# Small operands of the reciprocal roots and of the rows' maxima placed in unused columns of PSUM banks

## The chip, the cores and the metric

The kernel runs on one core of a Trainium2 chip, in one launch. The metric is the device time of one execution in microseconds, here 2229.23 us as the median of three runs (2226.55 to 2230.64).

The engines by the names of the profile: PE multiplies matrices (PEld are its weight loads), DVE is VectorE, ACT is ScalarE, POOL is GpSimd, SP issues the DMAs. SBUF is the memory on the chip that all of them work in. PSUM holds eight banks of 512 f32 columns on 128 partitions, into which PE writes its products; ACT and DVE read them from there. Each engine runs its own instructions in order and waits at semaphores for those of other engines.

## The reference

Two layers of a streaming encoder work on 1152 tokens (1024 of a prompt, and 8 requests of 16 samples) of 1024 channels, in f32. Layer 0 has a sliding-window attention and a recurrent branch (RG-LRU) side by side, layer 1 a gated MLP over chunks of 128 tokens; an MLP with a squared ReLU follows each.

```python
def rms_norm(x, g):
    xf = x.astype(jnp.float32)
    y = xf * lax.rsqrt(jnp.mean(xf * xf, axis=-1, keepdims=True) + EPS)
    return (y * g.astype(jnp.float32)).astype(x.dtype)
...
def softmax_with_sink(s, sink):
    sk = sink.astype(jnp.float32)[:, :, None, None]
    m = jnp.maximum(jnp.max(s, axis=-1, keepdims=True), sk)
    e = jnp.exp(s - m)
    return e / (jnp.sum(e, axis=-1, keepdims=True) + jnp.exp(sk - m))
...
    q = rope(rms_norm(q, q_g), pos)
    k = rope(rms_norm(k, k_g), pos)
...
    xc, new_buf = causal_conv(xr, conv_buf, conv_w, conv_b)
    hs, new_h = rg_lru(xc, h0, wa, ba, wx, bx, lam)
    rec = hs * jax.nn.gelu(gr)
    out = jnp.concatenate([att, rec], axis=-1) @ w_out
```

The reciprocal roots of the change are those of `rms_norm`: over the 1024 channels of a token ahead of each layer and each MLP, and over the 64 channels of each head of q and k. The rows' maxima are `jnp.max(s)` of the softmax.

## The kernel before

Every f32 product is made of three in a narrower format: weights and activations are split into a high part, rounded, and a low part, the rest (`three`, L526 to L528: high by high, low by high, high by low). The high part of a weight is a copy by ACT (`w<-raw`, L200), the low one a subtraction by DVE (L201); activations are split in `norm_split` (ACT L522, DVE L523). Weights come from HBM by DMA into `raw` in the order in which they are used.

The channels are laid on the partitions, and the tokens along the columns in three blocks of 384 (`nb`). These stages follow each other, with the times of the profile:

- **The start (0 to about 165 us).** The list `START` names the first steps: `n` splits a piece of x, `s` squares it and adds it to the sum over the channels, `w` splits a weight, `m` a projection, `f` is `stat_tokens`, `F` is `spread_stat`, `e` moves a projection out of PSUM. `stat_tokens` (L479) sums the squares over the partitions by three matmuls with one column each, into columns 0 to 2 of a bank of the kind `ax`, computes 1/1024 of that plus epsilon into the buffer `small`, and calls `rsqrt` (L446), which leaves the root of three times 128 tokens in `rT`. `spread_stat` (L495) turns it by PE into rows, and DVE copies them into `rstd`. Then the recurrent branch runs over four blocks of 128 channels (order in `LRU_ORDER`): projections, a causal convolution over 1176 columns (`add_conv`, L573), gate matmuls into `ax` banks (L526, `ax<-xch,w`), sigmoids and exponentials by ACT, a scan along the time by DVE (L644), and the product with a gelu. `prepare_lru` (L546) makes the constants `spc` of the decay out of 25 small instructions, also in `small`.
- **The attention (165 to 345 us).** Nine tiles of 128 tokens. `tile_steps` (L801) handles one of them: ACT copies q (eight heads of 64) and k and v out of two banks of the kind `mm` into `raw`, scaled; POOL squares q and k (ten heads); DVE sums each head (`tensor_reduce`), then takes ten roots per token by shift, subtraction from a constant, and three steps of Newton; POOL works meanwhile on the rotary embedding; DVE scales, and the result is split, transposed by PE and used for the scores. `prompt_steps` (L937) handles two heads of a tile: scores into a bank of the kind `qk`, DVE takes the maxima `mx` and from them the negative bound `nm`, ACT the exponentials with their sums, DVE the reciprocal, POOL the product, PE transposes, ACT and DVE split (`pT`), PE multiplies by v (`pv`), ACT and DVE split the result (`xn0h`, `xn0l`).
- **The out-projection** with the residual (to about 428 us), the statistics of the sum, and the **MLP**, whose products (L1293) take two thirds of the time. Then **layer 1**, from 1120 us on: gated MLP, out-projection, MLP. Their roots come from `stat_tokens` (L1152, L1184) and, for the layer norm of the gated MLP, from `rsqrt` with operands in SBUF.

What sets the order: a scheduler places the instructions of the start, the out-projections and the MLPs on each engine by its own estimate of when their inputs are ready, so that a changed dependence reorders others. In the attention the calls go through `InOrder`, which keeps the order in which the program makes them on each engine (all such instructions carry the line L257). That order is given by hand: `TILE_AT`, `REC_AT` and `PAIR_AT` list the due time of each step of a tile, of the recurrent rest and of a pair of heads; a step ends at each `yield`, and the steps of all of them are sorted by due time. A buffer can be written anew when its last reader has finished; so can a bank. Three `mm` banks serve q, and k and v, in turn.

The small operands of the root of a tile are ten columns each in one SBUF tile `st8`:

```python
        ss, v, y, w = (st8[:, 10 * i:10 * i + 10] for i in range(4))
```

(in the profile `st`), and those of the softmax are pairs of columns in `m`. The bank of k and v is filled in its first 256 columns of 512 (`kv_mm`); in a bank of scores columns 192 to 255 stay unused, since a chunk's scores take 192 (`pwide`).

Of the kernel before, what the change touches and what calls it, by code (L numbers as in the profile page):

```python
# [12 lines left out]
I32 = mybir.dt.int32  # L13
AF = mybir.ActivationFunctionType
OP = mybir.AluOpType
# [4 lines left out]
P = 128  # L20
# [261 lines left out]
def body(ctx, tc, io):  # L282
    nc = tc.nc
# [96 lines left out]
    q, kv = io["wq"], io["wkv"]  # L380
# [62 lines left out]
    rT = cp.tile([P, TT], F32, name="rT")  # L443
    small = cp.tile([P, 3, 16], F32, name="small")

    def rsqrt(y, v, t):  # L446

        yi, vi = y.bitcast(I32), v.bitcast(I32)
        nc.vector.tensor_scalar(yi, vi, 1, None, OP.logical_shift_right)
        nc.vector.tensor_scalar(yi, yi, -1, 0x5F3759DF, OP.mult, OP.add)  # L450
        for _ in range(3):
            nc.vector.scalar_tensor_tensor(t, y, -0.5, y, OP.mult, OP.mult)
            nc.vector.tensor_mul(t, t, v)
            nc.vector.scalar_tensor_tensor(y, t, 1.5, y, OP.add, OP.mult)


    ssum = {}
# [21 lines left out]
    def stat_tokens(nb, tag="ax"):  # L479

        s = ssum.pop(nb)
        ps = bank(tag)
        n = NBW // P
        for t in range(n):
            nc.tensor.matmul(ps[:, t:t + 1], s[:, t * P:t * P + P], ones, start=True, stop=True)
        v, w, r = small[:, 0, 0:n], small[:, 1, 0:n], rT[:, nb * n:nb * n + n]
        nc.vector.tensor_scalar(v, ps[:, 0:n], 1.0 / D, EPS, OP.mult, OP.add)
        rsqrt(r, v, w)

# [218 lines left out]
    for step in START.split():  # L708
# [11 lines left out]
        elif kind == "m":  # L720
            c, nb = n
# [6 lines left out]
    for kind, c in LRU_ORDER:  # L728
        if kind == "G":
            gates(c)  # L730
        else:
            nb = seen[kind, c] = seen.get((kind, c), -1) + 1
# [9 lines left out]
    PEo, ACTo, DVEo, POOLo = (InOrder(tc, e) for e in (nc.tensor, nc.scalar, nc.vector, nc.gpsimd))  # L742

    def at(name, shape, dt=F32, tag=None, bufs=1):
        return ap_.tile(shape, dt, tag=tag or name, bufs=bufs, name=name)
# [13 lines left out]
    raw = at("raw", [P, 12, 64])  # L759
# [6 lines left out]
    zero = pb[0][:, 0:NVV * 128].rearrange("p (n j x) -> p n j x", n=NVV, j=2)  # L766
    for a in (64, 128):
        nc.vector.tensor_copy(vv[:, :, :, a:a + 64], zero)
    st8 = at("st8", [P, 40])

    qkv = {}

# [28 lines left out]
    def tile_steps(s):  # L801
# [5 lines left out]
        r = rT[:, s:s + 1]  # L807
        ACTo.activation(raw[:, 0:8, :], qkv.pop(("q", s)).rearrange("p (h x) -> p h x", x=64), AF.Copy, scale=r)
        yield
        ACTo.activation(raw[:, 8:12, :], qkv.pop(("kv", s))[:, :256].rearrange("p (h x) -> p h x", x=64), AF.Copy, scale=r)  # L810
        yield
        qk = raw[:, 0:10, :]
        POOLo.tensor_mul(t1, qk, qk)
        yield
        ss, v, y, w = (st8[:, 10 * i:10 * i + 10] for i in range(4))
        DVEo.tensor_reduce(ss, t1, AX.X, OP.add)
        DVEo.tensor_scalar(v, ss, 1.0 / 64, EPS, OP.mult, OP.add)
        yield
# [4 lines left out]
                f = slice(32 - 32 * half, 64 - 32 * half)  # L823
                POOLo.tensor_mul(t2[:, a:b, o], qk[:, a:b, f], tab[:, i, 1:2, o].to_broadcast([P, n, 32]))
        yield
        yi, vi = y.bitcast(I32), v.bitcast(I32)
        DVEo.tensor_scalar(yi, vi, 1, None, OP.logical_shift_right)
        DVEo.tensor_scalar(yi, yi, -1, 0x5F3759DF, OP.mult, OP.add)
        for n in range(3):
            DVEo.scalar_tensor_tensor(w, y, -0.5, y, OP.mult, OP.mult)  # L830
            DVEo.tensor_mul(w, w, v)
            DVEo.scalar_tensor_tensor(y, w, 1.5, y, OP.add, OP.mult)
            if n == 1:
                yield
        yield
        for i, (a, b) in enumerate(((0, 8), (8, 10))):
            POOLo.tensor_mul(t1[:, a:b], qk[:, a:b], tab[:, i, 0:1, :].to_broadcast([P, b - a, 64]))
        yield
# [98 lines left out]
    def prompt_steps(t, i):  # L937

        kvh, pair = i % 2, i // 2
        h0 = kvh * 4 + pair * 2  # L940
        ps = bank("qk")
        p = pb[(4 * t + i) % NPB]
        qT = qTs[t % 2]
        for c in range(2):
            for a, n, pos in cells(t, c):
                o = ps[:, c * 256 + a:c * 256 + a + n]
                lhs = qT[:, c * 512 + h0 * 64:c * 512 + h0 * 64 + P]
                PEo.matmul(o, lhs, kT[:, kvh, 0, pos:pos + n], start=True, stop=False)
                PEo.matmul(o, lhs, kT[:, kvh, 1, pos:pos + n], start=False, stop=True)
        yield  # L950
        m = at(f"m{t}_{i}", [P, 8], tag="m", bufs=4)
        mx, nm, den, es = (m[:, 2 * k:2 * k + 2] for k in range(4))
        first = cells(t, 0)[0][0]
        spans = [(first, 192), (256 + max(first, 64), 512)]
        if t:
            DVEo.tensor_reduce(mx, pwide(ps), AX.X, OP.max)
        else:
            for c in range(2):
                DVEo.tensor_reduce(mx[:, c:c + 1], ps[:, spans[c][0]:spans[c][1]], AX.X, OP.max)
        DVEo.tensor_scalar(nm, mx, -0.125, nsink[:, h0 // 2:h0 // 2 + 1], OP.mult, OP.min)  # L960
        yield
        for c in range(2):
            a, b = spans[c]
            ACTo.activation(p[:, a:b], ps[:, a:b], AF.Exp, bias=nm[:, c:c + 1], scale=0.125,
                            accum_out=den[:, c:c + 1])
        ACTo.activation(es, nm, AF.Exp, bias=sink[:, h0 // 2:h0 // 2 + 1])
        yield
        DVEo.tensor_add(den, den, es)
        DVEo.reciprocal(den, den)
        yield  # L970
        if t:
            w = pwide(p)
            POOLo.tensor_mul(w, w, den.rearrange("p (c x) -> p c x", x=1).to_broadcast([P, 2, 192]))
        else:
            for c in range(2):
                a, b = spans[c]
                POOLo.tensor_scalar_mul(p[:, a:b], p[:, a:b], den[:, c:c + 1])
        yield
        pT = pTs[i % 2]
        ps = bank("tp")  # L980
        kts = (0, 1) if t else (1,)
        for kt in kts:
            for c in range(2):
                PEo.transpose(ps[:, (kt * 2 + c) * P:(kt * 2 + c + 1) * P],
                              p[:, c * 256 + kt * P:c * 256 + kt * P + P], ident)
        yield
        a = 256 * kts[0]
        ACTo.copy(pT[:, 0, a:], ps[:, a:])
        yield
        DVEo.tensor_sub(pT[:, 1, a:], ps[:, a:], pT[:, 0, a:].bitcast(F32))  # L990
        yield
        if kvh == 0:
            pv[0] = bank("pv")
        ps = pv[0]
        for kt in kts:
            vh, vl = (vv[:, (t - 1 + kt) % NVV, j, kvh * 128:kvh * 128 + 128] for j in range(2))
            ph, pl = (pT[:, j, kt * 256:kt * 256 + 256] for j in range(2))
            PEo.matmul(ps[:, :256], vh, ph, start=kvh == 0 and kt == kts[0], stop=False)
            PEo.matmul(ps[:, :256], vl, ph, start=False, stop=False)
            PEo.matmul(ps[:, :256], vh, pl, start=False, stop=kvh == 1 and kt == 1)  # L1000
        yield
        if kvh:
            src = ps[:, :256].rearrange("p (c j x) -> p j c x", c=2, j=2)
            cols = slice(t * P, t * P + P)
            o = [x[:, pair * 2:pair * 2 + 2, cols].rearrange("p j (c x) -> p j c x", c=2) for x in (xh, xl)]
            ACTo.copy(o[0], src)
        yield
        if kvh:
            DVEo.tensor_sub(o[1], src, o[0].bitcast(F32))
        yield  # L1010
# [95 lines left out]
    x = {}  # L1106
# [699 lines left out]
```

## Time and profile before

| what | us |
|---|---|
| median of three runs | 2229.23 |
| the profiled execution | 2230.83 |
| its span, first to last instruction | 2229.1 |
| PE busy in the span | 2167.5 |
| DVE busy | 1633.8 |
| ACT busy | 961.2 |
| POOL busy | 275.8 |

The span cut into 40 equal slices of some 56 us, the busy tenths of each engine in each:

```profile
PE   7988989899999999999999999989999999999999
DVE  7878984698777778777784644269877777877776
ACT  4665553367666642111152113226766665221211
POOL 4156641100000000000040333110000000000000
```

The first three slices are the start, the next three and a bit the attention and what follows it; POOL is busy there, and once more in the middle of layer 1 (slices 21 to 27). In between lie the MLPs, where PE is at nine tenths or more. How rows are read: start or count, busy time, engine, line, operation, output<-inputs, partitions x elements; a bracket gives the idle time of the engine ahead of the instruction and what ended it.

### The profile page before, as it was taken

How to read it: one execution, taken by the hardware profiler on the slowest of the kernel's cores; microseconds unless marked ns; L12 is line 12 of the kernel's file. 1: busy time of each engine (PE TensorE's matmuls, PEld its weight loads, DVE VectorE, ACT ScalarE, POOL GpSimd, SP SyncE). 2: the span in 40 equal slices, each digit the busy share in tenths (PEclk: the TensorE clock that was granted, in tenths of full speed). 3: DMA queues.
4: the chain of work that ended last, by engine and by line, in shares of the span. 5: the costliest groups of instructions: out<-in, count | busy, mean ns of one | idle time of the engine just before them, and what ended most of it. 6: DMA issues, size and time to landing. Idle time of an engine off the chain costs nothing.

```text
span 2229.1 us, 37892 instructions
## 1 busy us (share of the span) xinstructions
PE 2167.5 (97%) x14980; PEld 2120.6 (95%) x14980; DVE 1633.8 (73%) x2810; ACT 961.2 (43%) x1694; POOL 275.8 (12%) x332
## 2 busy tenths in 40 slices
PE   7988989899999999999999999989999999999999
PEld 7987889899999999999997899989999999999999
DVE  7878984698777778777784644269877777877776
ACT  4665553367666642111152113226766665221211
POOL 4156641100000000000040333110000000000000
PEclk9999999999999999999999999999999999999999
DMA  4120042227666677356652022422856667735573
GB/s 155 53 63 6 6 135 95 77 77 306 226 241 225 253 300 288 132 200 217 252 178 64 18 67 85 133 73 73 309 218 241 222 255 305 282 133 214 201 255 147
DMA packets 108002, 377.91 MB, mean 170 GB/s; under 512 B 13472, under 2 KB 24736, under 8 KB 107808
## 3 DMA queue, kind: packets, MB, share of 16 engines
q1 hardware_dynamic: 107680, 375.47, 46.9%
q8 instruction: 118, 1.93, 0.4%
q14 instruction: 60, 0.49, 0.1%
q10 hardware_dynamic: 144, 0.02, 0.0%
HBM read 240.09 MB, written 136.26 MB: 169 GB/s over the span
## 4 chain that ended last, share of the span: by engine, by line
PE 85%; DVE 9%; ACT 3%; issue 1%; DMA 1%; POOL 0%; SPq 0%; DVEq 0%; ACTq 0%; POOLq 0%
PE two L1293 64%; PE mm L527 4%; PE mm L526 4%; PE mm L528 4%; DVE st L257 2%; PE mm L1610 1%; PE mm L1612 1%; PE mm L1611 1%; PE mm L257 1%; DVE w L201 1%; DVE m L257 1%; PE pv L257 1%; PE ax L1639 1%; DVE y L573 1%; PE tp L257 1%
## 5 line engine op out<-in xcount | busy, mean ns | idle before, releaser
L1293 PE MATMUL two<-b,w 128*128 128x288 f32 x5424 | 727.8, 296 | 11.2 <-DVE x L1137 11.2
L1293 PEld LDWEIGHTS two<-b,w 128*128 128x128 f32 x5424 | 726.6, 189 | 11.7 <-issue 11.7
L1293 PE MATMUL two<-h,w 128*128 128x288 f32 x4704 | 630.6, 295 | 2.7 <-DVE x L1492 1.6
L1293 PEld LDWEIGHTS two<-h,w 128*128 128x128 f32 x4704 | 627.5, 188 | 4.5 <-issue 2.3
L200 ACT CAST w<-raw 128x512 fp32r<-128x512 f32 x542 | 331.7, 621 | 645.3 <-PE two L1293 435.8
L201 DVE TENSOR_TENSOR w<-raw,w 128x512 fp32r<-128x512 f32 x542 | 377.4, 701 | 107.7 <-ACT w L200 105.8
L1492 DVE TENSOR_TENSOR x<-two,x 128x576 f32<-128x576 f32 x448 | 336.1, 754 | 130.4 <-PE two L1293 129.1
L526 PE MATMUL mm<-xn0h,w 128*128 128x384 f32 x372 | 127.9, 344 | 7.0 <-ACT xn0h L522 6.5
L527 PE MATMUL mm<-xn1l,w 128*128 128x384 f32 x372 | 125.8, 338 | 1.7 <-DVE xn1l L523 1.7
L526 PE MATMUL mm<-xn1h,w 128*128 128x384 f32 x372 | 126.0, 339 | 0.0
L528 PE MATMUL mm<-xn0h,w 128*128 128x384 f32 x372 | 126.0, 339 | 0.0
L527 PE MATMUL mm<-xn0l,w 128*128 128x384 f32 x372 | 125.9, 339 | 0.0
L528 PE MATMUL mm<-xn1h,w 128*128 128x384 f32 x372 | 125.9, 338 | 0.0
L1542 POOL TENSOR_TENSOR s<-s,tmp 128x384 f32<-128x384 f32 (+1 forms) x28 | 29.1, 1064 | 729.1 <-ACT tmp L1541 728.8
L1293 PE MATMUL two<-hk,w 128*128 128x288 f32 x672 | 91.2, 295 | 0.0
L407 DVE TENSOR_TENSOR ho<-c_a,ho 128x576 fp32r<-128x576 f32 x78 | 57.2, 753 | 46.1 <-ACT ho L406 46.1
L1293 PEld LDWEIGHTS two<-hk,w 128*128 128x128 f32 x672 | 90.1, 188 | 0.0
L526 PEld LDWEIGHTS mm<-xn0h,w 128*128 128x128 f32 x372 | 71.0, 191 | 8.6 <-ACT xn0h L522 7.4
L1322 ACT ACTIVATE c_a<-c_a 128x1152 f32<-128x1152 f32 x60 | 70.1, 1168 | 14.8 <-DVE c_a L1404 13.8
L407 DVE TENSOR_TENSOR ho<-c_b,ho 128x576 fp32r<-128x576 f32 x96 | 72.3, 753 | 3.6 <-ACT ho L406 3.6
L1137 DVE TENSOR_TENSOR x<-mm,x 128x384 f32<-128x384 f32 x48 | 26.6, 554 | 64.6 <-PE mm L528 64.5
L527 PEld LDWEIGHTS mm<-xn1l,w 128*128 128x128 f32 x372 | 70.7, 190 | 2.1 <-DVE xn1l L523 2.0
(280 smaller groups left out, 2837.2 us busy)
## 6 DMA issues: line engine op xcount, KB each, us to landing
hidden<-ho SPq DMA_DIRECT2D x196, 576.0 KB, 4.0
h<-hidden SPq DMA_DIRECT2D x196, 576.0 KB, 6.3
raw<-in_w SPq DMA_DIRECT2D x136, 512.0 KB, 4.4
x<-scratch SPq DMA_DIRECT2D x24, 576.0 KB, 7.7
scratch<-x SPq DMA_DIRECT2D x48, 192.0 KB, 1.8
raw<-in_wo SPq DMA_DIRECT2D x16, 512.0 KB, 3.7
xin<-in_xT SPq DMA_DIRECT2D x24, 192.0 KB, 4.1
x<-in_xT SPq DMA_DIRECT2D x8, 576.0 KB, 3.8
```

Source lines behind the costliest of these rows:

```text
L200: nc.scalar.copy(t[:, 0], src)
L201: nc.vector.tensor_sub(t[:, 1], src, t[:, 0].bitcast(F32))
L257: return lambda *a, **k: self.tc.keep_in_program_order(op(*a, **k))
L407: nc.vector.tensor_sub(lo, src, hi.bitcast(F32))
L526: nc.tensor.matmul(ps, wh, ah, start=start, stop=False)
L527: nc.tensor.matmul(ps, wh, al, start=False, stop=False)
L528: nc.tensor.matmul(ps, wl, ah, start=False, stop=stop)
L1137: nc.vector.tensor_add(o, ps[:, :NBW], o)
L1293: nc.tensor.matmul(o, w, a[:, c], start=first and k == 0 and i == 0, stop=k == len(pairs) - 1 and i == 2, skip_group_check=True)
L1322: nc.scalar.activation(o, o, AF.Relu) if fn == "relu" else nc.scalar.square(o, o)
L1492: nc.vector.tensor_add(o, both(ps), o)
L1542: nc.gpsimd.tensor_add(o, o, sq)
```

## The change

`rsqrt` becomes a generator, `rsqrt_steps`, that takes the engine and yields behind the second and third step of Newton, as the hand-written copy of it in `tile_steps` did. The number of instructions is the same: a shift, a multiply-and-add, and three times three. What is new is which operands they have. Before, the step was t = −y/2 · y, t = t · v, y = (t + 1.5) · y; now it is t = −y/2 · v, t = t · y, y = (t + 1.5) · y, so that each instruction has `y` and just one of `v` and `t`. And `v` and `t` move to PSUM: in `stat_tokens` to columns 8 to 10 and 16 to 18 of the bank that holds the sums (before: `small`), in `tile_steps` with the sum of squares to columns 256, 272 and 288 of the bank of k and v (before: `st8`), while `y` is an SBUF tile of its own. The maxima `mx` move to columns 192 and 193 of the bank of scores. The layer norm's call of `rsqrt` keeps its operands in SBUF.

A bank is thereby held longer: that of k and v until the root ends, that of the sums too. `small` is left to `prepare_lru` and the scans.

```diff
     def rsqrt(y, v, t):
-        yi, vi = y.bitcast(I32), v.bitcast(I32)
-        nc.vector.tensor_scalar(yi, vi, 1, None, OP.logical_shift_right)
-        nc.vector.tensor_scalar(yi, yi, -1, 0x5F3759DF, OP.mult, OP.add)
-        for _ in range(3):
-            nc.vector.scalar_tensor_tensor(t, y, -0.5, y, OP.mult, OP.mult)
-            nc.vector.tensor_mul(t, t, v)
-            nc.vector.scalar_tensor_tensor(y, t, 1.5, y, OP.add, OP.mult)
+        for _ in rsqrt_steps(y, v, t, nc.vector):
+            pass
+
+    def rsqrt_steps(y, v, t, dve):
+        dve.tensor_scalar(t.bitcast(I32), v.bitcast(I32), 1, None, OP.logical_shift_right)
+        dve.tensor_scalar(y.bitcast(I32), t.bitcast(I32), -1, 0x5F3759DF, OP.mult, OP.add)
+        for n in range(3):
+            dve.scalar_tensor_tensor(t, y, -0.5, v, OP.mult, OP.mult)
+            dve.tensor_mul(t, t, y)
+            dve.scalar_tensor_tensor(y, t, 1.5, y, OP.add, OP.mult)
+            if n:
+                yield
...
-        v, w, r = small[:, 0, 0:n], small[:, 1, 0:n], rT[:, nb * n:nb * n + n]
+        v, w, r = ps[:, 8:8 + n], ps[:, 16:16 + n], rT[:, nb * n:nb * n + n]
...
-    st8 = at("st8", [P, 40])
+    y = at("y", [P, 10])
...
-        ACTo.activation(raw[:, 8:12, :], qkv.pop(("kv", s))[:, :256].rearrange("p (h x) -> p h x", x=64), AF.Copy, scale=r)
+        kvb = qkv.pop(("kv", s))
+        ACTo.activation(raw[:, 8:12, :], kvb[:, :256].rearrange("p (h x) -> p h x", x=64), AF.Copy, scale=r)
...
-        ss, v, y, w = (st8[:, 10 * i:10 * i + 10] for i in range(4))
+
+        ss, v, w = (kvb[:, 256 + 16 * i:266 + 16 * i] for i in range(3))
...
-        yi, vi = y.bitcast(I32), v.bitcast(I32)
...
-        yield
+        for _ in rsqrt_steps(y, v, w, DVEo):
+            yield
...
-        m = at(f"m{t}_{i}", [P, 8], tag="m", bufs=4)
-        mx, nm, den, es = (m[:, 2 * k:2 * k + 2] for k in range(4))
+        m = at(f"m{t}_{i}", [P, 6], tag="m", bufs=4)
+        nm, den, es = (m[:, 2 * k:2 * k + 2] for k in range(3))
+        mx = ps[:, 192:194]
```

The lines behind the diff's first part stand five further down in the changed kernel (L523 is L528 there, L644 is L649). In the attention the order of the instructions on each engine stays. At the start the scheduler reorders. First DVE at the end of the root of the first block (`small` and `rT` are the root's operands before, `ax_301` and `rT` now; L523 splits pieces of x, L496 copies the spread root). Before:

```order
L453 TENSOR_TENSOR small<-small 128x3
L454 SCALAR_TENSOR_TENSOR rT<-small,rT 128x3
L523 SCALAR_TENSOR_TENSOR xn1l_84<-xin_101,gt,xn1h_83 128x384
L523 SCALAR_TENSOR_TENSOR xn0l_79<-xin_97,gt,xn0h_78 128x384
L496 COPY rstd_88<-ax_376 128x384
```

Now:

```order
L528 SCALAR_TENSOR_TENSOR xn1l_84<-xin_101,gt,xn1h_83 128x384
L455 SCALAR_TENSOR_TENSOR ax_301<-rT,ax_301 128x3
L528 SCALAR_TENSOR_TENSOR xn0l_79<-xin_97,gt,xn0h_78 128x384
L456 TENSOR_TENSOR ax_301<-ax_301,rT 128x3
L528 SCALAR_TENSOR_TENSOR xn1l_84<-xin_99,gt,xn1h_83 128x384
L457 SCALAR_TENSOR_TENSOR rT<-ax_301,rT 128x3
L201 TENSOR_TENSOR w_415<-raw_163,w_415 128x512
L201 TENSOR_TENSOR w_418<-raw_163,w_418 128x512
L501 COPY rstd_88<-ax_376 128x384
```

Three splits of x stand between the last instructions of the root, and two splits of a weight behind it, ahead of the copy. `prepare_lru`, which also writes `small`, stood behind the root of block 1 (from row 81 of DVE's on) and now stands ahead of it (rows 56 to 80). Next, DVE around the first scan (`h_754<-rg_722,rg_738`; `u_784` is a projection for the gelu, `pad_718` the next block's convolution input). Before:

```order
L631 SCALAR_TENSOR_TENSOR h_754<-rg_722,h_754 128x1176
L634 TENSOR_TENSOR rg_738<-rg_738,h_754 128x1176
L641 MEMSET rg_722 128x8
L640 TENSOR_TENSOR rg_738<-rg_738,small 128x8
L644 SCALAR_TENSOR_TENSOR h_754<-rg_722,rg_738 128x1176
L691 TENSOR_TENSOR u_784<-mm_864,rstd_88 128x384
L201 TENSOR_TENSOR w_517<-raw_506,w_517 128x512
L674 TENSOR_TENSOR pad_718<-mm_897,rstd_88 128x256
```

Now:

```order
L636 SCALAR_TENSOR_TENSOR h_754<-rg_722,h_754 128x1176
L696 TENSOR_TENSOR u_784<-mm_864,rstd_88 128x384
L201 TENSOR_TENSOR w_517<-raw_506,w_517 128x512
L639 TENSOR_TENSOR rg_738<-rg_738,h_754 128x1176
L201 TENSOR_TENSOR w_545<-raw_515,w_545 128x512
L201 TENSOR_TENSOR w_548<-raw_515,w_548 128x512
L645 TENSOR_TENSOR rg_738<-rg_738,small 128x8
L646 MEMSET rg_722 128x8
L679 TENSOR_TENSOR pad_718<-mm_897,rstd_88 128x256
L649 SCALAR_TENSOR_TENSOR h_754<-rg_722,rg_738 128x1176
```

The projection, three splits of weights and the padding, behind the scan before, stand ahead of it. Last, PE at the gate matmuls of the sixth bank (`ax_858`). Before:

```order
L526 MATMUL mm_897<-xn1h_83,w_464 128x384
L527 MATMUL mm_897<-xn1l_84,w_464 128x384
L526 MATMUL ax_858<-xch_814,w_503 128x392
L527 MATMUL ax_858<-xcl_816,w_503 128x392
L528 MATMUL ax_858<-xch_814,w_503 128x392
L528 MATMUL mm_897<-xn1h_83,w_464 128x384
```

Now:

```order
L531 MATMUL mm_984<-xn1h_83,w_512 128x384
L532 MATMUL mm_984<-xn1l_84,w_512 128x384
L533 MATMUL mm_984<-xn1h_83,w_512 128x384
L531 MATMUL ax_858<-xch_814,w_503 128x392
L532 MATMUL ax_858<-xcl_816,w_503 128x392
L533 MATMUL ax_858<-xch_814,w_503 128x392
L531 MATMUL mm_1017<-xn0h_78,w_545 128x384
```

They stood in the middle of the projection `mm_897`, at row 372 of PE's; they now stand at row 400, behind a whole further projection, `mm_984`. On SP the order of the DMAs is the same but for a few outputs of the cache.

More of the change, by code (lines that the diff above doesn't have):

```diff
@@ L825, in tile_steps @@
         yield
-        yi, vi = y.bitcast(I32), v.bitcast(I32)
[L827 to L833, printed above, removed]
-                yield
-        yield
+        for _ in rsqrt_steps(y, v, w, DVEo):
+            yield
         for i, (a, b) in enumerate(((0, 8), (8, 10))):
```

## The prediction

> **What bounds the kernel now.** I read the page first: the share of each engine, then the chain of work that ended last.
>
> ```profile
> span 2229.1 us, 37892 instructions
> PE 85%; DVE 9%; ACT 3%; issue 1%; DMA 1%; POOL 0%; SPq 0%; DVEq 0%; ACTq 0%; POOLq 0%
> PE two L1293 64%; PE mm L527 4%; PE mm L526 4%; PE mm L528 4%; DVE st L257 2%; PE mm L1610 1%; PE mm L1612 1%; PE mm L1611 1%; PE mm L257 1%; DVE w L201 1%; DVE m L257 1%; PE pv L257 1%; PE ax L1639 1%; DVE y L573 1%; PE tp L257 1%
> ```
>
> TensorE ends 85% of the chain, and the products of the MLPs (L1293) alone 64%; the change touches none of those. But VectorE's small instructions on `st` and `m` (L257), which it does touch, hold 3% of the chain, some 65 us. So I read next how busy the engines are in each stage. The columns are the stretch, its length, then busy time and count of PE, weight loads, DVE, ACT and POOL, then the granted clock, the DMA share and GB/s.
>
> ```profile
> 60.00:165.00 105.00, 94.27 (x510) 90.74 (x509) 81.50 (x101) 70.75 (x86) 35.76 (x30) 0.95 0.21 61
> 165.00:285.00 120.00, 109.75 (x754) 97.40 (x753) 108.39 (x276) 66.89 (x219) 75.11 (x95) 0.99 0.03 8
> 285.00:345.00 60.00, 53.87 (x341) 50.78 (x341) 51.28 (x131) 34.84 (x109) 21.23 (x25) 0.91 0.42 133
> 450.00:1120.00 670.00, 669.40 (x5019) 668.69 (x5018) 529.19 (x790) 302.36 (x467) 0.00 (x0) 1.00 0.62 229
> ```
>
> From 450 to 1120 us PE has no gap: nothing is to be won or lost there. From 165 to 285 us, in the attention, PE is idle for 120 − 109.75 = 10.25 us while VectorE is 108.4 of 120 us busy. What PE waits for there, in the waits of PE (total, times, longest):
>
> ```profile
> PE pv L257 <- DVE xn0l L257: 6.2, 5, 1.7
> PE tp L257 <- DVE xa L257: 3.5, 3, 2.1
> ```
>
> 9.7 of the 10.25 us are waits for VectorE. So in this stage VectorE sets the end, with PE close behind it. That caps the gain: however much VectorE is relieved, PE's own 109.75 us remain.
>
> **What the change does to VectorE.** The timeline of one tile's root (start, length, engine):
>
> ```profile
> 228.94 1.71 POOL L257 TENSOR_TENSOR rstd<-raw,tab 128x512 f32<-128x512 f32 x2
> 228.99 1.70 DVE L257 TENSOR_SCALAR st<-st 128x10 int32<-128x10 int32 x2
> 230.73 1.58 POOL L257 TENSOR_TENSOR rstd<-rstd,rope_b 128x640 f32<-128x640 f32 x1
> 230.92 1.42 DVE L257 TENSOR_TENSOR st<-st 128x10 f32<-128x10 f32 x1
> 232.38 0.38 DVE L257 SCALAR_TENSOR_TENSOR st<-st 128x10 f32<-128x10 f32 x2
> ```
>
> Ten elements per partition take 1.4 us as long as a POOL instruction runs: the one that starts at 230.92 ends at 232.34, just behind the POOL instruction's end at 232.31; with POOL done, two take 0.38. I look for which instructions this happens to, in the groups (count, busy us, mean ns) and in the summaries of three buffers (shortest, median and longest ns):
>
> ```profile
> L257 DVE SCALAR_TENSOR_TENSOR st<-st 128x10 f32<-128x10 f32 x54 | 21.2, 392 | 1.5
> L257 DVE TENSOR_TENSOR st<-st 128x10 f32<-128x10 f32 x27 | 11.4, 423 | 0.9
> L257 DVE TENSOR_SCALAR st<-st 128x10 int32<-128x10 int32 x18 | 9.9, 548 | 0.3
> L257 DVE TENSOR_SCALAR m<-m,nsink 128x2 f32<-128x2 f32 x32 | 14.3, 448 | 1.0
> L257 DVE TENSOR_SCALAR m<-m,nsink x32: 216/478/1000, 179.8 to 326.4; 128x2 f32<-128x2 f32 x32
> L257 DVE SCALAR_TENSOR_TENSOR st<-st x54: 148/170/1425, 166.6 to 316.9; 128x10 f32<-128x10 f32 x54
> L257 DVE TENSOR_TENSOR pT<-tp,pT x16: 410/681/693, 191.9 to 339.0; 128x512 fp32r<-128x512 f32 x14, 128x256 fp32r<-128x256 f32 x2
> ```
>
> The undisturbed price is about 168 ns (the median of the first kind is 170). Instructions with both operands in SBUF are stretched to 1425; the subtraction `pT<-tp,pT`, which has one operand in PSUM and is fifty times larger, never goes above 693 among the same POOL work. So I take it that an instruction with one operand in PSUM goes free of POOL. The change gives every instruction of the tile's root such an operand, and the maxima's `nm` too. What goes: 54 × (392 − 168) = 12.1, 27 × (423 − 168) = 6.9, 18 × (548 − 168) = 6.8, 32 × (448 − 220) = 7.3 us (220 being an undisturbed `nm`, whose shortest is 216): **33 us of VectorE's time**, 3.7 us in each of nine tiles. That is more than the waits it can end.
>
> What of it shortens the span: the 9.7 us of waits, plus slowed work just behind them:
>
> ```profile
> 206.44 0.83 PE L257 MATMUL pv<-xa,vv 128*128 128x256 f32 x5
> 252.14 1.25 PE L257 MATMUL pv<-xa,vv 128*128 128x256 f32 x6 [1.19 <-DVE xn0l L257]
> 168.30 1.58 POOL L257 TENSOR_TENSOR rstd<-rstd,rope_b 128x640 f32<-128x640 f32 x1
> 171.25 0.17 DVE L257 SCALAR_TENSOR_TENSOR st<-st 128x10 f32<-128x10 f32 x1
> ```
>
> Six of these after a stall take 1.25 us; five without one 0.83, so six would take 1.0: 0.25 us for each of the five stalls, 1.3 together. Sum 11.0. I take off 1.5. In the first tile, whose stall is the 2.1, POOL's own sum is late next: it ends at 169.88, 1.5 us before the root, so 0.6 stays. The other 0.9 is an allowance for waits behind which ACT stands. **Attention: −9.5 us**, bounds −6 (half the waits find another engine) and −14 (some of the 6.1 us that PE idles from 285 to 345 too, though those mostly wait for ACT and weights).
>
> What holds longer: the root's operands lie in the bank of k and v, which now comes free at the end of the root, not after ACT's copy. The next user of such a bank is a projection two tiles later:
>
> ```profile
> 170.80 0.63 PE L257 MATMUL mm<-w,xn0h 128*128 128x512 f32 x2
> 234.66 0.72 DVE L257 SCALAR_TENSOR_TENSOR st<-st 128x10 f32<-128x10 f32 x1
> 239.65 0.63 PE L257 MATMUL mm<-w,xn0h 128*128 128x512 f32 x2
> ```
>
> In a middle tile the root ends at 235.4, the matmuls start at 239.65: 4 us to spare. In the first tile the root ends at 171.42 (its last row is above), the matmuls start at 170.80; there they would wait 0.6 us, but about 3.5 us of stretching go before that point. Cost 0.
>
> The price of the PSUM operand itself. Reading:
>
> ```profile
> L487 DVE TENSOR_SCALAR small<-ax x10: 151/160/161, 26.7 to 1483.3; 128x3 f32<-128x3 f32 x10
> L449 DVE TENSOR_SCALAR rT<-small x12: 151/168/218, 26.9 to 1506.8; 128x3 int32<-128x3 int32 x12
> ```
>
> From PSUM 160 ns, from SBUF 168: no charge. Small results that VectorE writes to PSUM are not in the trace. Bounds: nothing, as for reads, up to 0.2 us an instruction (a second access as long as a whole small one). I take 0, the value of the nearest row. Below nothing isn't excluded either, but 8 ns × 21 instructions a tile is 0.2 us and hides.
>
> [...]
>
> **The start (0 to 165 us)** is a chain of latencies: first root, gates, four scans, first tile. Here the change also reorders, as the order of VectorE and PE shows.
>
> ```profile
> 28.40 0.97 DVE L453 TENSOR_TENSOR small<-small 128x3 f32<-128x3 f32 x1
> 33.51 0.92 DVE L454 SCALAR_TENSOR_TENSOR rT<-small,rT 128x3 f32<-128x3 f32 x1
> 34.49 1.65 PE L495 MATMUL ax<-ident,rT 128*128 128x128 f32 x6 [4.21 <-DVE rT L454]
> 47.15 0.16 DVE L487 TENSOR_SCALAR small<-ax 128x3 f32<-128x3 f32 x1 [5.49 <-PE ax L485]
> 72.46 2.72 DVE L560 TENSOR_SCALAR small<-small 128x4 f32<-128x4 f32 x1
> 76.67 1.28 ACT L619 ACTIVATE h<-rg,spc 128x1176 f32<-128x1176 f32 x1 [3.27 <-DVE spc L565]
> 87.39 2.61 DVE L644 TENSOR_TENSOR_SCAN h<-rg,rg 128x1176 f32<-128x1176 f32 x1
> 92.03 0.70 PE L526 MATMUL ax<-xch,w 128*128 128x392 f32 x1 [3.17 <-ACT rg L608]
> 92.52 0.69 DVE L201 TENSOR_TENSOR w<-raw,w 128x512 fp32r<-128x512 f32 x1 [2.07 <-ACT w L200]
> ```
>
> Three pieces. *The first root*: five of its small instructions take 0.85 to 0.97 in place of 0.16, some 3.7 us, and PE waits 4.21 for its end at 34.43. Now they are free, but three subtractions of 128x384 stand between its last step's instructions, 0.6 us each alone and 1.3 beside POOL: −3.7 + 1.8 to +3.9, and these go on meeting POOL, which adds from 30 to 37 us. I take +2 (bounds −1.5 and +5.3). *The decay's constants* (L551 to L565) no longer wait for the buffer `small` that block 1's root used; they go into VectorE's 5.49 us of idleness before 47.15, and ACT's wait of 3.27 for `spc` goes: −3.3. *The first scan* now stands behind `u`, three weights' subtractions and the padding. A subtraction takes 0.69; by that price, for four of the five (one fits into a wait), +2.7. The conv ahead of it gets two more instructions of that size and a half: +1.7, an estimate. In the three later gate blocks weights' subtractions leave VectorE's part, three in the first of them, and a gelu enters ACT's: −0.9 each by the same price, an estimate, −2.6. The gate matmuls at 92.03, which stalled PE 3.17, now stand behind a whole projection, which fills that gap; as the scans set the pace there, I count nothing for it. Altogether +2 − 3.3 + 2.7 + 1.7 − 2.6 = **+0.5 us**, bounds −3 and +5. This is the least certain term: its pieces have rows, their sum along a scheduler's new order has none.
>
> **Later roots.** In the two out-projections and before the MLPs POOL doesn't run beside the roots, so nothing is won. Their last step now shares VectorE with other work:
>
> ```profile
> 426.25 0.93 PE L495 MATMUL ax<-ident,rT 128*128 128x128 f32 x6
> ```
>
> PE doesn't stall there now; the root ends about 1.3 us later and the copy behind it moves, while a weight's subtraction (0.7) and a sum (0.56) leave the part behind: +0.2 at each of four or five places, **+1** (0 to +3). The roots of the gMLP lie beside PE at full load: 0.
>
> Sum: −9.5 + 0.5 + 1 = −8 us. The profiled execution took 2230.83 us (span 2229.1), 1.6 above the median 2229.23 of the three runs; made against its own time, 2230.83 − 8 = 2222.8, which I give as 2222.5.
>
> **Rivals.** 0.2%, 4.5 us, is about what a measurement of this kernel can tell from no change: faster means below 2224.8, slower above 2233.7.
> - *The start eats it.* If the three subtractions meet POOL in full (+5.3) and the first scan is held as reckoned, the start is +5 and the later roots +3: −9.5 + 8 = −1.5, 2229. For: the interleaved rows stand in the order, and the first root is on the chain. Against: ACT's wait of 3.27 for `spc` goes. 0.16.
> - *A small price of PSUM.* Say a third of the upper bound, 0.07 us for each instruction with a PSUM operand. VectorE gives back 1.5 of 3.7 us a tile and the waits mostly go still: −8. The instructions of a root follow from each other, so in the five roots on the chain (the first, and two at each out-projection) 5 × 11 × 0.07 = 3.9 are added: −8 + 3.9 + 0.5 + 1 = −2.6, 2228. Against it stand 160 and 168 ns; for it, that those are reads alone. 0.10. [...]
> - *Writing PSUM is dear (the slower side).* Most results of the new root go to PSUM, and the next instruction waits for them. From 3.7 / 21 = 0.18 us a write, VectorE has lost in the attention what it won, and PE's waits are back. At 0.2 us the 55 instructions of the five roots add 11, the attention 0: 2230.83 + 11 + 0.5 + 1 = 2243. For: no row shows such a write. Against: reads cost nothing. 0.07.
> - *VectorE isn't freed.* If it isn't the PSUM operand that spares `pT<-tp,pT`, the stretching stays: 2230.83 + 0.5 + 1 = 2232. The 693 ns of its longest speak against it. 0.02.
>
> **How the numbers follow.** The forecast has 0.65, the rivals 0.16, 0.10, 0.07, 0.02. The bounds of its three terms, taken as independent, spread the forecast from about −13 to −2 around −8, so 0.05 of its 0.65 lies within 0.2%; of the small price 0.02 falls below 2224.8, of the bad start 0.01 above 2233.7, as of the last. Faster 0.60 + 0.02 = 0.62, same 0.05 + 0.08 + 0.15 + 0.01 = 0.29, slower 0.07 + 0.02 = 0.09. The range reaches down to 2214 (the attention at −14, the start at −3) and up to 2232, which takes in the bad start, the small price and the case in which nothing is freed, and leaves out the dear write.
>
> **What would show it.** In the new profile the root's instructions in the tiles should have mean and median alike near 170 ns and PE's waits for VectorE from 165 to 285 us should fall below 2 us; the next late would be ACT. The start's part shows alone in when the first scan (87.39 now) and the first tile's root (its end at 171.42) come. Instructions of 230 ns or more would show a price of PSUM. I am wrong if POOL stretches them still, or if the first tile comes more than 5 us later.

## The result and the profile after

The changed kernel takes **2215.02 us** (median of four runs, 2212.70 to 2215.67), against 2228.73 before (four runs, 2226.55 to 2230.64): a ratio of 0.9938, with a 95% interval of 0.9922 to 0.9953. It is faster by 13.7 us; the forecast was 2222.5, and 2215.02 lies inside its range, 1 us above the lower end of 2214.

The page of the changed kernel, its span and the chain of work that ended last, and then the windows and PE's waits in the attention, with the columns as before:

```profile
span 2213.9 us, 37892 instructions
PE 88%; DVE 6%; ACT 2%; issue 2%; DMA 1%; POOL 1%; SPq 0%; ACTq 0%; DVEq 0%; POOLq 0%
60.00:165.00 105.00, 92.89 (x504) 89.16 (x503) 78.84 (x87) 73.37 (x87) 34.42 (x30) 0.95 0.18 57
165.00:285.00 120.00, 116.13 (x817) 105.04 (x815) 102.15 (x301) 73.38 (x237) 84.91 (x104) 1.00 0.07 20
285.00:345.00 60.00, 55.42 (x380) 52.78 (x381) 47.64 (x133) 36.99 (x123) 20.49 (x27) 1.00 0.40 135
PE tp L257 <- DVE xa L257: 2.8, 2, 1.8
PE pv L257 <- DVE xn0l L257: 0.2, 1, 0.2
```

In the window from 165 to 285 us PE is now busy for 116.1 us in place of 109.8, and it does more of the work there (817 matmuls, before 754). VectorE's share of the chain fell from 9 to 6%. The timeline of a root in a middle tile shows why:

```profile
225.27 1.71 POOL L257 TENSOR_TENSOR rstd<-raw,tab 128x512 f32<-128x512 f32 x2
225.37 0.17 DVE L257 TENSOR_SCALAR y<-mm 128x10 int32<-128x10 int32 x1
225.58 0.17 DVE L257 SCALAR_TENSOR_TENSOR mm<-y,mm 128x10 f32<-128x10 f32 x1
225.79 0.18 DVE L257 TENSOR_TENSOR mm<-mm,y 128x10 f32<-128x10 f32 x1
226.00 0.17 DVE L257 SCALAR_TENSOR_TENSOR y<-mm,y 128x10 f32<-128x10 f32 x1
227.06 1.56 POOL L257 TENSOR_TENSOR rstd<-rstd,rope_b 128x640 f32<-128x640 f32 x1
228.00 0.64 DVE L257 TENSOR_TENSOR m<-m 128x2 f32<-128x2 f32 x1 [0.28 <-ACT m L257]
```

Four steps of the root run at 0.17 to 0.18 us under a POOL row of 1.71 (two instructions one behind the other). The last row is one that the change leaves with two operands in SBUF: it starts at 228.00 under a POOL instruction, and ends just behind that one's end at 228.62. The groups of such instructions (count, busy us, mean ns):

```profile
L257 DVE SCALAR_TENSOR_TENSOR mm<-y,mm 128x10 f32<-128x10 f32 x27 | 4.5, 168 | 0.6
L257 DVE SCALAR_TENSOR_TENSOR y<-mm,y 128x10 f32<-128x10 f32 x27 | 4.5, 168 | 0.9
L257 DVE TENSOR_TENSOR mm<-mm,y 128x10 f32<-128x10 f32 x27 | 4.7, 176 | 0.9
L257 DVE TENSOR_SCALAR m<-qk,nsink 128x2 f32<-128x2 f32 x32 | 7.0, 217 | 1.0
L257 DVE TENSOR_TENSOR m<-m 128x2 f32<-128x2 f32 x32 | 11.2, 349 | 2.8 <-ACT m L257 2.6
```

The first four are where the prediction put them (392, 423 and 448 ns before). The fifth, the sum of the denominator, rose from 179 to 349. PE's waits for VectorE from 165 to 285 us came down from 9.7 to 3.0 us, not below 2 as the prediction asked for.

To compare stages I take four points: the first matmul of the token statistics (`ax<-ones`, which itself moves by up to 1.5 us from profile to profile), the sum of squares of the first and of the ninth tile, and the first matmul of the MLP. The start of each:

| stage (us) | before | after | difference |
|---|---|---|---|
| first statistics matmul | 25.28 | 24.55 | −0.7 |
| from there to the first tile | 139.36 | 143.21 | **+3.9** |
| first to ninth tile | 142.78 | 128.42 | **−14.4** |
| ninth tile to the first MLP | 132.84 | 130.52 | −2.3 |
| the rest | 1788.84 | 1787.20 | −1.6 |
| span | 2229.10 | 2213.90 | −15.2 |

The attention gave 16.7 us with its last tile, and the start took 4 back. How far such a stage varies by itself: in the seven profiles below and above whose start has the order of before (in one of them but for a few of VectorE's small instructions), the second line lies between 137.3 and 139.4. In three with the token roots of the start in PSUM it lies between 141.6 and 143.2.

### The profile page after: what moved, and what is told of

Same layout as the page of the kernel before. It is cut to its first block, busy times and chain, and to the rows that moved or that the text cites. A ratio compares the mean times of both kernels' runs of the same rounds, so it can differ in the third digit from the quotient of the medians.

```text
span 2213.9 us, 37892 instructions
## 1 busy us (share of the span) xinstructions
PE 2157.8 (97%) x14980; PEld 2114.9 (96%) x14980; DVE 1614.8 (73%) x2810; ACT 961.8 (43%) x1695; POOL 279.4 (13%) x332
## 4 chain that ended last, share of the span: by engine, by line
PE 88%; DVE 6%; ACT 2%; issue 2%; DMA 1%; POOL 1%; SPq 0%; ACTq 0%; DVEq 0%; POOLq 0%
PE two L1293 64%; PE mm L533 5%; PE mm L531 5%; PE mm L532 5%; PE mm L257 2%; PE mm L1610 1%; PE mm L1612 1%; PE mm L1611 1%; DVE w L201 1%; PE pv L257 1%; PE tp L257 1%; PE ax L1639 1%; PE qk L257 1%; DVE b L407 0%; DVE x L1492 0%
## 5 line engine op out<-in xcount | busy, mean ns | idle before, releaser
L201 DVE TENSOR_TENSOR w<-raw,w 128x512 fp32r<-128x512 f32 x542 | 386.4, 718 | 113.7 <-ACT w L200 111.5
L480 POOL TENSOR_TENSOR s<-s,tmp 128x384 f32<-128x384 f32 x49 | 54.7, 1121 | 148.2 <-ACT tmp L478 146.0
```

The lines of the kernel that those rows point to most:

```text
L201: nc.vector.tensor_sub(t[:, 1], src, t[:, 0].bitcast(F32))
L480: (nc.vector if sum_on_dve else nc.gpsimd).tensor_add(ssum[nb], ssum[nb], sq)
```

## The experiments

Each was timed beside the kernel before on the same chip, whose medians there were 2226.8 to 2227.8. "First tile" is the second line of the table, "tiles" the third.

**One half of the change each.** The attention's edits alone (`tile_steps`, `prompt_steps`; the token roots stay as before):

```diff
-        v, w, r = ps[:, 8:8 + n], ps[:, 16:16 + n], rT[:, nb * n:nb * n + n]
+        v, w, r = small[:, 0, 0:n], small[:, 1, 0:n], rT[:, nb * n:nb * n + n]
```

(against the changed kernel; `rsqrt` in its old form)

> Only the attention's part of the change (root of the tile in the bank of k and v, new form of Newton's step, maxima in the bank of scores); the token statistics keep small and the old form, so that the order of the first 165 us is that of before. Theory A (the gain comes whole from the attention, the start's new order costs 3.1): first tile's sum of squares at 164.6 as before, first to ninth tile 128.4 us in place of 142.8, and about 2212 us, faster than the whole change. Rival B (the start's order has no cost of its own, it only shifts work out of the attention): the attention gains only some 11, 2215 to 2217.

Measured: 2211.63 us, ratio 0.9932 (0.9920 to 0.9945); first tile 138.14 (at 162.77), tiles 128.44, ninth tile to MLP 130.51, as with the whole change. The other half, the same pieces of the diff exchanged:

> Only the token statistics and rsqrt changed; the attention as before. Theory A: first tile's sum of squares 3.1 us later (167.8), first to ninth tile 142.8 as before, layer 1 up to 1.6 shorter, total 2229 to 2232. Rival B: 2226 or less, the attention then shorter than 142.8.

Measured: 2231.08, ratio 1.0017 (1.0008 to 1.0026), slower beyond its interval; first tile 141.60 (at 166.77), tiles 142.37. So theory A holds: the whole gain comes from the attention, and the token roots cost some 4 us (2231.08 against 2226.79 for the kernel before beside it; in the first tile 2 to 4 us, by the spread given above).

**What in the attention.** The root alone (the maxima back in `m`):

> Only the root of the tiles in PSUM with its new form; the maxima stay in SBUF, the token statistics are as before. The root's stretching was 26 of 33 us of VectorE's excess, the maxima's 7. Theory A1 (VectorE sets the pace until PE has no more gaps, so the last part frees nothing that counts): 85% or more of the attention's gain, first to ninth tile 129 to 131. Rival (each share of VectorE's time counts alike): 132 to 133. nm stays at 448 ns or more.

Measured: 2212.33, ratio 0.9935 (0.9922 to 0.9947); tiles 127.93, ninth tile to MLP 132.02, 259.95 together against 258.95 with the maxima and 275.6 before. The root brings nearly all. `nm` rose from 448 to 526 ns: it meets POOL more now that the root doesn't wait ahead of it, which is argued from the order and not tested. Next, the new form of the step and the tile `y` alone:

```diff
-        ss, v, w = (kvb[:, 256 + 16 * i:266 + 16 * i] for i in range(3))
+        ss, v, w = (st8[:, 10 * i:10 * i + 10] for i in range(3))
```

> The new form of Newton's step and the tile y of its own, but sum, v and t of the tile's root stay in SBUF, the maxima and the statistics too. Theory A (the operand in PSUM is what spares the instruction POOL's wait): the root's instructions stay at means of 390 to 550 ns, first to ninth tile 142 to 143, 2228 to 2231, no change. Rival C (the form, or y apart from v and t, does it): means near 170 and some 2215.

Measured: 2226.42, ratio 1.0000 (0.9991 to 1.0009); tiles 142.46. Its groups:

```profile
L257 DVE SCALAR_TENSOR_TENSOR y<-st,y 128x10 f32<-128x10 f32 x27 | 13.7, 506 | 0.9
L257 DVE TENSOR_TENSOR st<-st,y 128x10 f32<-128x10 f32 x27 | 10.1, 376 | 0.9
L257 DVE SCALAR_TENSOR_TENSOR st<-y,st 128x10 f32<-128x10 f32 x27 | 8.8, 326 | 0.6
L257 DVE TENSOR_SCALAR y<-st 128x10 int32<-128x10 int32 x9 | 6.7, 745 | 0.3
```

Same arithmetic in the same order as the changed kernel, with the operands in SBUF: means of 326 to 745 ns in place of 167 to 176, and no gain. From the kernel with the root alone (2212.33) this one differs in nothing but the place of these operands. It is the place that counts. The new form is what lets each instruction have just one operand in PSUM. And the maxima alone:

```diff
-        mx, nm, den, es = (m[:, 2 * k:2 * k + 2] for k in range(4))
+        nm, den, es = (m[:, 2 * k:2 * k + 2] for k in range(3))
+        mx = ps[:, 192:194]
```

> Only the maxima in PSUM. They came to 7.3 of 33 us of stretching. Theory A (each us of VectorE's counts while VectorE sets the pace): first to ninth tile 136 to 139, 2221 to 2224. Rival D (the wait for POOL moves on to the sum behind it, whose mean went from 179 to 349 ns in the whole change): 141 to 143, less than 2 us.

Measured: 2226.03, ratio 0.9995 (0.9986 to 1.0004); tiles 143.69. Rival D in the time, though the tiles lie a little above its 141 to 143 and the wait moved on to other instructions than it named:

```profile
L257 DVE SCALAR_TENSOR_TENSOR st<-st 128x10 f32<-128x10 f32 x54 | 25.4, 470 | 1.5
L257 DVE TENSOR_SCALAR st<-st 128x10 int32<-128x10 int32 x18 | 12.3, 684 | 0.3
L257 DVE TENSOR_TENSOR st<-st 128x10 f32<-128x10 f32 x27 | 6.5, 242 | 0.9
L257 DVE TENSOR_SCALAR m<-qk,nsink 128x2 f32<-128x2 f32 x32 | 7.0, 218 | 1.0
```

`nm` fell from 14.3 us to 7.0, while the root's four groups rose from 45.1 to 46.9 us (the fourth, 128x10 f32, is 2.7) and the split `xa` of 128x512 from 6.1 to 7.7. Freeing the maxima alone handed part of their wait to the root and the splits, and won nothing.

**The wait that was left.** The sink's exponential also goes to the bank of scores, on top of the attention's edits alone, so that the denominator's sum has one operand in PSUM:

```diff
-        nm, den, es = (m[:, 2 * k:2 * k + 2] for k in range(3))
-        mx = ps[:, 192:194]
+        nm, den = (m[:, 2 * k:2 * k + 2] for k in range(2))
+        mx, es = ps[:, 192:194], ps[:, 196:198]
```

> The attention's part alone, and the sink's exponential too lies in the bank of scores, so that the sum of the denominator has one operand in PSUM (345 ns now). Theory A (PE is the bound by now, it idles only 6 of 128 us): VectorE wins 5.5 us, the time 0 to 3 us, 2209 to 2212. Rival: the bank of scores is held until that sum, PE waits for it: 2213 or more.

Measured: 2210.05, ratio 0.9920 (0.9906 to 0.9933); the sum takes 152 ns in place of 345, tiles 126.35 in place of 128.44, ninth tile to MLP 129.62 in place of 130.51. PE is busy for 123.0 of those 126.35 us: at most 3.3 us of waits for VectorE are left here. In the medians (2211.63 with the attention alone) this is within the intervals; the stages show it.

**What the start loses.** First the constants of the decay, which the change moves ahead. A buffer of their own, with the attention's edits alone:

```diff
+    lsm = cp.tile([P, 2, 16], F32, name="lsm")
-        a, e, z, z2, s = (small[:, 0, 4 * i:4 * i + 4] if i < 4 else small[:, 1, 0:4] for i in range(5))
+        a, e, z, z2, s = (lsm[:, 0, 4 * i:4 * i + 4] if i < 4 else lsm[:, 1, 0:4] for i in range(5))
```

> The attention's part of the change alone, and the constants of the decay get a buffer of their own, so that they go ahead of block 1's root as in the whole change; the token roots stay in SBUF and end as before. Theory S1 (what the start loses comes from the token roots' operands in PSUM, by which the order puts splits of x between their last instructions; the early constants are a gain): the first tile's sum of squares comes 1 to 3 us earlier than with the attention alone (162.8, which is 138.1 after the first statistics matmul), 2209 to 2211. Rival S2 (the early constants displace the convolution and the scans and are the cost): 3 to 5 later, 2215.

Measured: 2212.60 (0.9931, 0.9918 to 0.9943); first tile 138.62, within the spread of that stage. Neither theory: the early constants are no gain and no cost. The copies of roots 2 and 3 came 2.6 and 3.9 us later, since 25 instructions now stand ahead of them, and the exponential that had waited for the constants started no earlier (50.6 us after the first statistics matmul, with the attention alone 50.2). The other way round, the whole change with the constants held back:

```diff
         rsqrt(r, v, w)
+        nc.vector.tensor_copy(small[:, 0, 0:n], r)
```

> The whole change, and behind each token root a small copy into small (12 more instructions of about 0.16 us), so that the constants of the decay come late again as before. Theory S1: the interleaved root stays and the early constants' gain goes: first tile 143 to 147 us after the first statistics matmul (143.2 with the whole change), 2215 to 2219. Rival S2: 138 to 140, some 2211.

Measured: 2215.05 (0.9942, 0.9928 to 0.9955); first tile 142.91, against 143.21 with the whole change. The constants' place is not the cost; the three token roots in PSUM are. Their instructions themselves became shorter (the 128x3 steps of the start take 159 to 166 ns on the mean in place of 248 to 328), so it is likely the new order that costs; no run has these roots in PSUM in the old order. Which of them, told by a condition in `stat_tokens` of the changed kernel: all three of the start back in `small`, then only the second and third, then only the first:

```diff
+        if stat.n <= 3:
+            v, w = small[:, 0, 0:n], small[:, 1, 0:n]
```

(`stat.n <= 3 and nb > 0` in the second, `stat.n <= 3 and nb == 0` in the third.)

> The whole change, but the three token roots of the start keep their operands in small (new form); the later token roots stay in PSUM. Theory S1: the start is as with the attention alone, first tile 138.1 to 138.5 us after the first statistics matmul, 2210 to 2213; and if the later roots cost the 1 us that was forecast, from the first MLP on 1 us more than the 1788.2 of the attention alone. Rival L (the later roots in PSUM are a gain of 1 to 1.6): 1787 or less there.

> As the one before, but the first token root of the start in PSUM too, only roots 2 and 3 of the start in small. The first root's end among splits of x costs 1.6 us at the first copy (12.5 in place of 10.9 after the first statistics matmul). If that delay runs through to the first tile: 139.7 to 140; if the order behind it (the scan behind a projection, the gates' matmuls 11 rows later) adds its own: 141 or more.

> The whole change, but the first token root in small; roots 2 and 3 in PSUM. First copy at 10.9 again. If the first root were the cause of the start's loss: first tile 138 to 139. If the order of roots 2 and 3 and of the scans behind them is (theory S1 in its second half): 141 to 143.

| token roots of the start in PSUM | median | ratio (95%) | first copy | first tile |
|---|---|---|---|---|
| none | 2212.17 | 0.9931 (0.9919 to 0.9944) | 10.92 | 137.61 |
| the first | 2208.17 | 0.9913 (0.9899 to 0.9926) | 12.39 | **134.45** |
| second and third | 2214.45 | 0.9944 (0.9930 to 0.9957) | 10.95 | 139.66 |
| all three (the change) | 2215.02 | 0.9938 (0.9922 to 0.9953) | 12.57 | **143.21** |

(copy and tile in us after the first statistics matmul). No theory foresaw the second line. The first root does end 1.5 us later, as predicted, and the first tile comes 3.2 us earlier nonetheless; the last kernel below, with the same start, has 134.45 again. A group in the profiles with none and with the first in PSUM shows the largest difference, the convolution's twelve instructions:

```profile
L580 DVE SCALAR_TENSOR_TENSOR y<-pad,lc,y 128x1176 f32<-128x1176 f32 x12 | 21.6, 1809 | 0.8 <-ACT y L577 0.8
L580 DVE SCALAR_TENSOR_TENSOR y<-pad,lc,y 128x1176 f32<-128x1176 f32 x12 | 17.2, 1435 | 0.9 <-ACT y L577 0.9
```

With none in PSUM two of them run into POOL's products of the branch before:

```profile
109.98 3.66 POOL L705 TENSOR_TENSOR h<-h,u 128x1024 f32<-128x1024 f32 x1 [13.47 <-issue]
111.39 3.49 DVE L580 SCALAR_TENSOR_TENSOR y<-pad,lc,y 128x1176 f32<-128x1176 f32 x1
117.10 2.73 POOL L635 TENSOR_TENSOR rg<-rg,y 128x1176 f32<-128x1176 f32 x1
117.23 3.84 DVE L580 SCALAR_TENSOR_TENSOR y<-pad,lc,y 128x1176 f32<-128x1176 f32 x1
```

They take 3.49 and 3.84 us, and each ends 1.24 us behind the POOL product under which it started; in the other order none starts under such a product, and the mean is 1.44. It looks like the same wait between POOL and two inputs in SBUF, now between large instructions, and the order decides who meets whom. The 4.4 us that this group saves are enough for the 3.2, and most of the time is won between the second and the third scan, which lie 19.9 us apart in place of 24.2. That these two waits are the cause is argued, not shown: with roots 2 and 3 in PSUM one instruction of the group still takes 3.58 us, and those scans lie 19.8 us apart. The kernels with roots 2 and 3 in PSUM, in which the group takes 19.4 us, have lost their time ahead of all that: their first scan starts 66.9 (all three) and 67.5 us after the first statistics matmul, against 60.2 with none in PSUM and 62.1 with the first. Which instruction of that order costs it is left open.

**The two best single edits together**: the first root of the start and all later ones in PSUM, the second and third in `small`, and the sink's exponential in the bank of scores.

> The first token root of the start and all later ones in PSUM, roots 2 and 3 in small, the attention as in the whole change, and the sink's exponential in the bank of scores: the two single best edits together. If both gains are real and lie in different stages they add: first tile 134 to 135 us after the first statistics matmul, first to ninth tile 126.4, 2206 to 2207, at most 2208. Rival (one of them was chance of a run): 2209 or more.

Measured: **2204.98** (2203.95 to 2205.61), ratio 0.9896 (0.9879 to 0.9912); first tile 134.45, tiles 126.71. The gains lie in different stages and add. Against the kernel before that ran beside it, this one is faster by 22.9 us, the change by 13.7.

## Why the prediction was right, point by point

**What bounds the kernel**: right. VectorE set the pace of the attention, PE close behind (129.57 and 128.44 us busy of the 142.78 between the first and the ninth tile). PE's idle time between the first and the ninth tile fell from 14.3 to 6.2 us. The 33 us of VectorE's time that the prediction frees did go (its four groups fell from 56.8 to 23.7 us), but the sum of the denominator rose from 5.7 to 11.2 us and three groups of large instructions by another 5.7 (`rope_b` of 128x640 7.4 to 9.3, `xn1l` of 128x512 5.4 to 7.7, `xa<-rope_b,xa` of 128x512 6.1 to 7.6): a third of the freed time was spent again.

**An instruction with one operand in PSUM goes free of POOL**: right, shown by the form-only kernel: 168 to 176 ns with one of two inputs in PSUM, 326, 376 and 506 with both in SBUF. The group of 745 ns has one input and its result in SBUF and is stretched too (167 with the input in PSUM). The reciprocal `m<-m` of 128x2 has its input and its result there as well, and took 168 ns at most in the kernel with the sink's exponential in PSUM, where 14 of its 32 started under a POOL instruction. What tells these two apart, no run shows.

**The price of PSUM, 0**: right within 10 ns, for writes too: `mm<-mm,y` reads and writes PSUM in 176 ns on the mean, and `st<-st`, the product with both operands in SBUF, had a median of 170 before; the sum over a head takes 817 ns into PSUM and took 807 into SBUF (medians). Both rivals on the price fall.

**Attention −9.5**: right mechanism, wrong size, and outside its own bound of −14: it measured −14.4 between the tiles and −2.3 behind them. Two terms of the sum were mis-sized: the slowed work behind the stalls, put at 1.3, and what lies behind 285 us, put at nothing. PE's idle time fell by 8.1 us over the eight tiles, and that this is close to the 8.2 (9.7 less 1.5) of the sum is luck: 3.5 of it were waits put down to ACT. The windows of the whole stretch, then of the first tile, of the six behind it and of the eighth, before:

```profile
164.64:307.42 142.78, 128.44 (x865) 114.18 (x863) 129.57 (x324) 82.60 (x266) 86.02 (x107) 0.96 0.10 28
164.64:178.07 13.43, 11.30 (x63) 9.61 (x62) 9.19 (x20) 3.71 (x9) 8.77 (x13) 0.87 0.02 6
178.07:281.69 103.62, 95.57 (x672) 85.17 (x671) 96.25 (x251) 61.33 (x206) 65.76 (x82) 1.00 0.02 6
281.69:307.42 25.73, 21.57 (x134) 19.40 (x133) 24.13 (x57) 17.56 (x53) 11.50 (x15) 0.87 0.43 127
```

and after:

```profile
167.76:296.18 128.42, 122.18 (x866) 110.63 (x865) 112.30 (x324) 82.46 (x264) 87.47 (x107) 1.00 0.09 29
167.76:178.81 11.05, 9.22 (x59) 7.83 (x58) 6.24 (x20) 3.76 (x9) 7.47 (x10) 1.00 0.03 7
178.81:273.18 94.37, 92.97 (x671) 85.23 (x670) 83.44 (x250) 61.52 (x206) 67.23 (x84) 1.00 0.02 6
273.18:296.18 23.00, 19.99 (x140) 17.58 (x139) 22.62 (x57) 17.18 (x51) 12.76 (x15) 1.00 0.41 130
```

In the six tiles in the middle, at a clock of 1.00 both times, PE's idle time fell by 6.7 us and its busy time for all but one of the same matmuls by 2.6, twice the 1.3 of the sum: some 0.4 us a tile. I had read that price from one row of six matmuls and looked no further than the row.

In the first and the eighth tile the granted clock was 0.87 before and is 1.00 now, and PE's busy time fell by 3.7. But for the time of the stage this counted little. The first tile of the form-only kernel, and the eighth of the kernel with the start's token roots in SBUF:

```profile
162.65:174.80 12.15, 9.86 (x62) 8.41 (x61) 9.18 (x19) 3.74 (x9) 7.48 (x10) 1.00 0.02 6
267.43:290.43 23.00, 21.18 (x140) 19.14 (x139) 22.70 (x57) 17.22 (x51) 12.78 (x15) 0.93 0.41 125
```

The first has the old stretching at a clock of 1.00: the tile is 1.3 us shorter than before, and the whole stage, 142.46, is shorter by 0.3. The second has a clock of 0.93 and takes the same 23.00 us as the changed kernel at 1.00. In the eighth tile VectorE was busy for 24.13 of 25.73 us before and 22.62 of 23.00 now: it sets the pace there too. That tile's 2.7 us and the 2.3 behind it are what the prediction put at nothing and named in its bound alone, since it read PE's waits behind 285 us as waits for ACT and weights. The first seven tiles gave 11.6.

**The start, +0.5**: too low. It is +3.9 against the profile of before, and +5.1 against the attention alone, whose start has the order of before; I had bounded it by +5. Step by step, against the profile of before: the first copy came 1.7 us later (predicted +2, although the pieces named for it, −3.7 and +1.8 to +3.9, give −1.9 to +0.2, and the rest was an allowance for POOL); the exponential that needs the constants 0.9 later, where +2 − 3.3 had been predicted; from it to the first scan 14.6 us instead of 10.7, +3.9 (predicted 4.4); the three blocks behind it, up to the fourth scan, −1.4 (predicted −2.6); and from there to the first tile +0.4. The step that failed is the constants, −3.3: I took a wait of ACT as gained, without asking what the 25 instructions push back where they go. They pushed back roots 2 and 3 (by 2.6 and 3.9 us in the kernel with the constants in a buffer of their own), and the gain was nothing there. The second error was to treat the pieces as a sum: with the first root alone in PSUM that root is late by 1.5 us and the first tile early by 3.2.

**Later roots, +1**: not seen. The first out-projection's stretch is the same with them in PSUM or SBUF (130.5). From the first MLP on, seven kernels with PSUM there lie between 1786.3 and 1788.7 us (the one with the start in SBUF at 1786.3), the seven without, that of before among them, between 1787.4 and 1788.9: a gain of some 0.6 on the mean, less than either group spreads.

**The bank held longer, 0**: right in the middle tiles: in the 94.37 us of the six, PE's idle time is 1.4 us, and its waits there are 1.0 for `xa` of VectorE and 0.4 for `xa` of ACT.

So −8 came out of −9.5 + 0.5 + 1, and −13.7 was measured (−15.2 between the two profiled executions); two errors of opposite sign, the larger on the gain.

## What to carry to other kernels

Small VectorE instructions that shared a stage with GpSimd here waited for it up to many times their own length when their operands lay in SBUF: products of 128x10 took up to 1491 ns, with a median of 170; unused columns of a PSUM bank that is held anyway were a free place for one operand, within 10 ns. Start with the groups that wait most, and look at what is left: the tile's root alone brought nearly all, the maxima alone nothing, and part of the freed time went to the next instructions with two inputs in SBUF (the sum of the denominator, 5.7 to 11.2 us). What TensorE gained here was more than its idle time: in the six middle tiles 6.7 us of that went, and with them 2.6 us of busy time for all but one of the same matmuls; and where a scheduler sets the order, take each part of an edit alone, since parts that look alike (root 1, and roots 2 and 3) can go opposite ways.

## What the hardware showed that I had not expected

That a slow stretch of PE behind a stall need not come from the stall. The same four transposes of the first tile, in the kernel before, in that with the new form alone and in that with the maxima alone:

```profile
173.78 0.74 PE L257 MATMUL tp<-identr,xa 128*128 128x128 f32 x4 [2.13 <-DVE xa L257]
171.78 0.54 PE L257 MATMUL tp<-identr,xa 128*128 128x128 f32 x4 [2.29 <-DVE xa L257]
170.62 0.53 PE L257 MATMUL tp<-identr,xa 128*128 128x128 f32 x4 [2.13 <-DVE xa L257]
```

Behind 2.13 us of waiting they take 0.74 us once and 0.53 the other time, and behind 2.29 us 0.54: the length of the wait just ahead doesn't decide it. What goes with the 0.74 is the clock. The window around these transposes in the kernel before has a granted clock of 0.50:

```profile
173.64:177.05 3.41, 3.27 (x16) 2.88 (x17) 0.78 (x4) 1.48 (x4) 1.89 (x2) 0.50 0.00 0
```

In the kernel with the new form alone the clock of that tile is 1.00. What lowered it in the one execution, no run here shows.
